# S5 chunks with rows ordered (input, place): inputs by two DMAs, outputs by four writes and four reads

## The chip, the core and the metric

The kernel runs on one core of one Trainium2 chip. The metric is the device time of one execution in microseconds (us). TensorE (PE) multiplies matrices and has its own weight-load track (PEld); VectorE (DVE), ScalarE (ACT) and GpSimd (POOL) do elementwise work. SyncE (SP) issues nearly all DMAs, one after the other: an issue that waits for a semaphore holds up those behind it. Each engine runs its instructions in the order in which they were put down.

## What is computed

One layer of a hybrid decoder for 256 prompt positions and 8 x 8 sample positions, 320 in all. A combined input projection feeds an S5 group and a retention group; both outputs go through one output projection, then a SwiGLU block. All in f32. The S5 part, which the change touches:

```python
    lam_bar = jnp.exp(lam_dt)
    b_bar = ((lam_bar - 1.0) / lam)[..., None] * b
    ug = uf.reshape(n, l, S5_GROUPS, S5_GROUP)
    bu = jnp.einsum('nlgh,gph->lngp', ug.astype(jnp.complex64), b_bar)
    bu = bu.at[0].add(lam_bar[None] * x0)
    _, xs = lax.associative_scan(_lin_combine, (a, bu), axis=0)
    y = jnp.einsum('lngp,ghp->nlgh', xs, c).real.reshape(n, l, S5_WIDTH)
    y = y + d.astype(f32) * uf
    y = jax.nn.gelu(y)
    y = y * jax.nn.sigmoid(y @ w_glu.astype(f32) + b_glu.astype(f32))
```

There are 64 groups of 16 channels; each group drives 64 complex states.

## The kernel before

**Matmuls.** Every large product is made of three f32r passes: weights are split into `hi` (rounded) and `lo` (the rest), activations likewise, and PE adds hi x hi, hi x lo, lo x hi (L143, L144, L145 in `gemm`; L161 to L163 in `gemm_late`). `wload` brings a block of weights, 128 x 1024: a DMA into `raw` on SP (L130), the cast to `hi` on ACT (L131), the subtraction to `lo` on DVE (L133). `raw`, `hi` and `lo` have three buffers each in the first part of the kernel, so a block's load waits until the `lo` three blocks earlier is made.

**Stages.** The input projection (up to about 343 us) has the retention heads and the S5 chunks woven into it. Then come the output projection for retention, the GLU of S5, the output projection for S5, and from about 490 us on the feed-forward block.

**Order.** PE and POOL run in the order of the code (L924): a clock with estimated costs (`clk`, `spawn`, `run_due`) decides there where a chunk's next part is put between matmuls. DVE, ACT and SP are ordered by a scheduler, which uses priorities (weight loads and PSUM evacuations come first) and its own estimates of when things are ready.

**One S5 chunk** (`s5_chunk`, eight of them, each of 128 channels, i.e. eight groups). Positions are taken in blocks of four (CH = 4), so there are 80 blocks (NC). The rows (partitions) of the operands are pairs of an input channel of the group (16, `h`) and a place in the block (4, `e`, `t` or `s`). Before, the order of a row is (place, input): place is the slower index.

- `up_` (ACT, L588) is the chunk's input regrouped; it is written to DRAM (`via`, L591) and read back with eight DMAs (L595) into `kst`, one for each half and place.
- `bl` and `cl` (DVE) are products of the raw B and C matrices (`raw_bc`) with powers of the state's multiplier (`gpc`, `lpc`). `gpc` is made once by ACT (`s5_powers`, L491 and L492).
- PE transposes `bl` into `bst`, multiplies `kst` with it into PSUM `pb`, and `bl` with `cl0` into `pk_`, from which ACT copies one column block of `toe` (L649). Six DMAs inside SBUF (L653) shift it by one, two and three places and complete the matrix `toe` of the block's inner effects.
- `s5_scan` (DVE) runs the recurrence over blocks and leaves `xp`.
- PE multiplies `toe` with `kst` and `cl` with `xp` into `py`; ACT and DVE evacuate it into `ev`. One DMA writes `ev` to DRAM (`back`, L682); eight DMAs read it into `yc` (L687) in the channels' own order.
- `y1` (DVE, L691; the profile shows it at the helper's line L182, `y<-u,vec,yc`) adds the direct term. Then come Square, Identity and Tanh on ACT (L693, L694, L696) with two more DVE operations, and the result goes back to `u32`, where the GLU stage finds it.

ACT is also what normalises the retention heads' outputs (`on`, L804), after DVE's statistics (L787, L788) and a chain of small POOL operations.

Of the kernel before, what the change touches and what calls it, by code (L numbers as in the profile page):

```python
# [12 lines left out]
F32 = mybir.dt.float32  # L13
# [4 lines left out]
ADD, SUB, MUL = ALU.add, ALU.subtract, ALU.mult  # L18
PSUM = bass.MemoryType.PSUM

P = 128
# [11 lines left out]
CH = 4  # L33
NCP = NP // CH
NC = N // CH
# [9 lines left out]
def hybrid_kernel(ctx, tc, xT, w_in, w_in4, w_out, w_glu, w_fi, w_fo, vecs, s5p, bc, x0,  # L45
# [24 lines left out]
    o = 0  # L70
# [34 lines left out]
    def tr(out, in_):  # L105
        m = in_.shape[0]
        pe.transpose(out, in_, ident[:m, :m])
        clk.now += 0.12
# [68 lines left out]
    def tt(out, a, b, op):  # L177
        dve.tensor_tensor(out, a, b, op)  # L178
        return out
# [305 lines left out]
    def s5_powers():  # L485
        for q in range(2):
            for d in range(2):
                o = lpc[:, :, q, 4 * d:4 * d + 4]
                act.mul(o, lp[:, q].rearrange("p e (c j) -> p c j e", j=4), -1.0 if d > q else 1.0)
                o = gpc[:, :, q, 4 * d:4 * d + 4]  # L490
                act.copy(o[:, :, :, 0], ff[:, q].rearrange("p (c j) -> p c j", j=4))  # L491
                act.copy(o[:, :, :, 1:], gp[:, q].rearrange("p e (c j) -> p c j e", j=4))  # L492

    def s5_turns(ec, es):
        pool.memset(e18[:, :, 0, :, 0:1], 1.0)
# [87 lines left out]
    def s5_chunk(c):  # L583
        js = slice(4 * c, 4 * c + 4)
        cl, cl0, xp, d0 = cls_[c % 2], cl0s[c % 2], xps[c % 2], d0s[c % 2]

        up_ = s5.tile([P, CH, NC], F32, name="up_", tag="up_", bufs=2)
        act.copy(up_, u32[:, c].rearrange("p (c s) -> p s c", s=CH))  # L588

        via = drm.tile([4, 2, 16, CH, NC], F32, name="via", tag="via", bufs=2)  # L590
        sp.dma_start(via.rearrange("j g h s c -> (j g h) (s c)"), up_.rearrange("p s c -> p (s c)"))  # L591
        kst = s5.tile([P, 4, NC], F32, name="kst", tag="kst", bufs=2)
        for i in range(2):
            for e in range(CH):
                sp.dma_start(kst[64 * i + 16 * e:64 * i + 16 * e + 16],  # L595
                             via[2 * i:2 * i + 2, :, :, CH - 1 - e].rearrange("q g h c -> h (q g) c"))

        raw = raws[c]
        for q in range(2):
            for g in range(2):  # L600
                act.mul(cl0[64 * g:64 * g + 64, q, :, 16 * g:16 * g + 16],
                        raw[64 * g:64 * g + 64, 1, 4 * q:4 * q + 4], 1.0 - 2.0 * q)
        with tc.issue_after(rot_t["values"].ins):
            act.copy(d0[:, :, :, 1:], r4[:, js].unsqueeze(1).unsqueeze(3).to_broadcast([P, 2, 4, NCP - 1]))
        shm = [P, 8, CH, 16]
        for w_, pc in ((0, gpc), (1, lpc)):
            m1, m2 = (s5.tile(shm, F32, name=f"m{q}", tag=f"m{q}", bufs=1) for q in range(2))
            b_ = raw[:, w_].unsqueeze(2).to_broadcast(shm)
            tt(m1, b_, pc[:, c, 0].unsqueeze(3).to_broadcast(shm), MUL)
            tt(m2, b_, pc[:, c, 1].unsqueeze(3).to_broadcast(shm), MUL)  # L610
            if w_ == 0:

                bl = s5.tile([P, 2, 2, 2, CH, 16], F32, name="bl", tag="bl", bufs=1)
                for r, (a, b, op) in enumerate(((m1[:, 0:4], m2[:, 4:8], SUB), (m1[:, 4:8], m2[:, 0:4], ADD))):
                    a, b = (t_.rearrange("p (u q) e h -> p u q (e h)", q=2) for t_ in (a, b))
                    tt(bl[:, r].rearrange("p q u e h -> p u q (e h)"), a, b, op)
                continue
            tt(cl[:, 0], m1[:, 0:4], m2[:, 4:8], SUB)
            tt(cl[:, 1], m1[:, 4:8], m2[:, 0:4], SUB)
        if c:  # L620
            tbl = s5_table(c)
        yield DL["b1"] + (4.0 if c == 0 else 0.0)
        if not c:
            tbl = s5_table(c)
        bst = s5.tile([P, 4, P], F32, name="bst", tag="bst", bufs=1)
        pt = misc("pt")
        for i in range(4):
            tr(pt[:, P * i:P * i + P], bl[:, i // 2, i % 2].rearrange("p u e h -> p (u e h)"))
        with tc.high_priority(offset=EVAC):
            act.copy(bst, pt.rearrange("p (i s) -> p i s", s=P))  # L630
        load_bc(c + 2)
        yield DL["b2"]
        pb = ps_b.tile([P, 2, 512], F32, name="pb", tag="pb", bufs=1)
        for i in range(4):
            for u in range(2):

                for g in range(2):
                    us, gs = slice(64 * u, 64 * u + 64), slice(64 * g, 64 * g + 64)
                    mm(0.04, pb[gs, u, NC * i:NC * i + NC], bst[us, i, gs], kst[us, 2 * (i % 2) + g],
                       start=True, stop=True, tile_position=(64 * u, 64 * g))  # L640
        pk_ = misc("pk_")
        for i in range(2):
            for q in range(2):
                for u in range(2):
                    mm(0.04, pk_[64 * u:64 * u + 64, 32 * i:32 * i + 32],
                       bl[:, q, i, u].rearrange("p e h -> p (e h)"), cl0[:, q, 2 * u + i],
                       start=q == 0, stop=q == 1, tile_position=(0, 64 * u))
        with tc.high_priority(offset=EVAC):
            act.copy(toe[:, :, CH - 1], pk_[:, 0:64].rearrange("p (q h) -> p q h", h=16))  # L649
        for u in range(2):  # L650
            for t in range(CH - 1):
                d = 16 * (CH - 1 - t)
                sp.dma_start(toe[64 * u + d:64 * u + 64, :, t], toe[64 * u:64 * u + 64 - d, :, CH - 1])  # L653
        with tc.high_priority(offset=2 * EVAC if c == 7 else 0):
            s5_scan(c, pb, xp, d0, tbl)
        yield DL["scan"]


        py = ps_b.tile([P, 2, 512], F32, name="py", tag="pb", bufs=1)
        for g in range(2):  # L660
            for u in range(2):
                for i in range(2):
                    us = slice(64 * u, 64 * u + 64)
                    mm(0.04, py[64 * i:64 * i + 64, u, NC * g:NC * g + NC],
                       toe[us, 2 * i + g].rearrange("p t h -> p (t h)"), kst[us, 2 * i + g], start=g == 0,
                       stop=True, tile_position=(64 * u, 64 * i), skip_group_check=True)
        for u in range(2):
            for q in range(2):
                for g in range(2):
                    for i in range(2):  # L670
                        gs = slice(64 * g, 64 * g + 64)
                        mm(0.04, py[64 * i:64 * i + 64, g, NC * (2 + u):NC * (3 + u)],
                           cl[gs, q, 2 * u + i].rearrange("p t h -> p (t h)"), xp[gs, q, 2 * u + i],
                           start=False, stop=q == 1, tile_position=(64 * g, 64 * i), skip_group_check=True)
        ev = s5.tile([P, 2, 2, NC], F32, name="ev", tag="ev", bufs=1)
        with tc.high_priority(offset=EVAC):
            act.copy(ev.rearrange("p u g c -> p u (g c)"), py[:, :, 0:2 * NC])
            tt(ev, ev,
               py[:, :, 2 * NC:4 * NC].rearrange("p g (u c) -> p u g c", c=NC), ADD)

        back = drm.tile([2, CH, 16, 2, 2, NC], F32, name="back", tag="back", bufs=2)
        sp.dma_start(back.rearrange("i t h u g c -> (i t h) (u g c)"), ev.rearrange("p u g c -> p (u g c)"))  # L682
        yc = s5.tile([P, CH, NC], F32, name="yc", tag="yc", bufs=1)
        for j in range(4):
            for g in range(2):
                r = 32 * j + 16 * g
                sp.dma_start(yc[r:r + 16], back[j % 2, :, :, j // 2, g].rearrange("t h c -> h t c"))  # L687
        yield DL["y"]
        y1 = s5.tile([P, N], F32, name="y1", tag="up_", bufs=2)
        y2 = s5.tile([P, N], F32, name="y2", tag="ev", bufs=1)  # L690
        stt(y1.rearrange("p (c s) -> p c s", s=CH), u32[:, c].rearrange("p (c s) -> p c s", s=CH),  # L691
            v("d", c), yc.rearrange("p s c -> p c s"), MUL, ADD)
        act.activation(y2, y1, AF.Square)  # L693
        act.activation(y2, y2, AF.Identity, scale=0.044715, bias=ones[:, 0:1])  # L694
        tt(y2, y2, y1, MUL)
        act.activation(y2, y2, AF.Tanh, scale=float(np.sqrt(2 / np.pi)))  # L696
        stt(u32[:, c], y2, 1.0, y1, ADD, MUL)
        if c == 7:
            s5_state["done"] = True
# [417 lines left out]
    for n in range(KT):  # L1117
# [8 lines left out]
        else:  # L1126
            s = square(n, hp)
# [216 lines left out]
```

## Time and profile before

| | us |
|---|---|
| median of 3 runs | 1434.91 (1433.25 to 1435.58) |
| the profiled execution | 1433.95 |
| its span, first to last instruction | 1432.1 |

The profile is of one execution, so its times are set against 1433.95 and not against the median. Weights and inputs come at a mean of 186 GB/s. The busy share of PE by slices of a fortieth of the span is 0.9 or more in all but the last:

```profile
PE   9999999999999999999999999999999999999996
...
DVE  7978887777567647776677546777644767644554
ACT  7645555554355433333333333333333333333452
POOL 7530022110000010000001000001000000000001
PEclk9999999999999999999999999999999999999998
DMA  8555555556544466675666446757445765444442
```

Each digit is tenths. The S5 chunks lie in slices 2 to 11. Matmuls are pipelined, so the durations of neighbouring rows overlap: two full matmuls start 0.147 us apart and are shown with 0.31 us each.

### The profile page before, as it was taken

To read this page: it belongs to the slowest core of one execution; us is meant where nothing else is said; L and a number is where in the kernel's file an instruction comes from. 1 tells how busy PE (TensorE), PEld (TensorE's weight loads), DVE (VectorE), ACT (ScalarE), POOL (GpSimd) and SP (SyncE) were. 2 spreads that over 40 slices of the span, in tenths; PEclk is the share of its full clock that TensorE was granted. 3 is DMA by queue.
4 is the path that set the end of the run, shared out by engine and by line. 5 is a ranking of instruction groups with operands and counts; after the bars stand their busy time and mean duration, and the time that the engine had idled before them with its cause. 6 is when DMAs were issued, how large, how long until landed. Compare 5 with 4: busy or idle time off the path is not lost.

```text
span 1432.1 us, 26209 instructions
## 1 busy us (share of the span) xinstructions
PE 1418.1 (99%) x10394; PEld 1407.6 (98%) x10394; DVE 954.6 (67%) x1853; ACT 598.8 (42%) x944; POOL 125.1 (9%) x193
## 2 busy tenths in 40 slices
PE   9999999999999999999999999999999999999996
PEld 9999999999999999999999999999999999999996
DVE  7978887777567647776677546777644767644554
ACT  7645555554355433333333333333333333333452
POOL 7530022110000010000001000001000000000001
PEclk9999999999999999999999999999999999999998
DMA  8555555556544466675666446757445765444442
GB/s 285 175 172 161 165 167 165 169 160 208 162 156 152 152 210 228 221 250 205 239 217 228 128 150 234 247 202 254 151 152 185 256 225 183 153 127 156 148 148 108
DMA packets 101803, 266.87 MB, mean 186 GB/s; under 512 B 27312, under 2 KB 41776, under 8 KB 101680
## 3 DMA queue, kind: packets, MB, share of 16 engines
q1 hardware_dynamic: 101536, 264.94, 55.7%
q8 instruction: 81, 1.33, 0.4%
q14 instruction: 42, 0.34, 0.1%
q10 hardware_dynamic: 144, 0.26, 0.1%
HBM read 254.24 MB, written 10.52 MB: 185 GB/s over the span
## 4 chain that ended last, share of the span: by engine, by line
PE 71%; DVE 1%; issue 0%; ACT 0%; DVEq 0%
PE ps_fu L144 7%; PE ps_fu L143 7%; PE ps_fo L143 7%; PE ps_fo L144 7%; PE ps_fo L145 7%; PE ps_fu L145 7%; PE ps_fg L144 7%; PE ps_fg L143 7%; PE ps_fg L145 7%; PE ps_o L145 1%; PE ps_o L143 1%; PE ps_o L144 1%; PE ps_g L144 1%; PE ps_g L145 1%; PE ps_g L143 1%; DVE x L178 0%
## 5 line engine op out<-in xcount | busy, mean ns | idle before, releaser
L131 ACT CAST hi<-raw 128x1024 fp32r<-128x1024 f32 (+1 forms) x416 | 402.2, 968 | 697.4 <-PE ps_fo L144 189.0
L133 DVE TENSOR_TENSOR lo<-raw,hi 128x1024 fp32r<-128x1024 f32 (+1 forms) x416 | 467.5, 1124 | 314.9 <-ACT hi L131 312.4
L144 PE MATMUL ps_fo<-alo,hi 128*128 128x320 f32 x704 | 217.5, 309 | 0.0
L143 PE MATMUL ps_fg<-hhi,hi 128*128 128x320 f32 x704 | 217.5, 309 | 0.0
L143 PE MATMUL ps_fo<-ahi,hi 128*128 128x320 f32 x704 | 217.5, 309 | 0.0
L145 PE MATMUL ps_fo<-ahi,lo 128*128 128x320 f32 x704 | 217.5, 309 | 0.0
L144 PE MATMUL ps_fu<-hlo,hi 128*128 128x320 f32 x704 | 217.4, 309 | 0.0
L145 PE MATMUL ps_fg<-hhi,lo 128*128 128x320 f32 x704 | 217.4, 309 | 0.0
L143 PE MATMUL ps_fu<-hhi,hi 128*128 128x320 f32 x704 | 217.4, 309 | 0.0
L144 PE MATMUL ps_fg<-hlo,hi 128*128 128x320 f32 x704 | 217.4, 309 | 0.0
L145 PE MATMUL ps_fu<-hhi,lo 128*128 128x320 f32 x704 | 217.4, 309 | 0.0
L143 PE MATMUL ps_p<-xhi,hi 128*128 128x320 f32 x560 | 177.3, 317 | 0.0
L145 PE MATMUL ps_p<-xhi,lo 128*128 128x320 f32 x560 | 173.0, 309 | 0.0
L144 PE MATMUL ps_p<-xlo,hi 128*128 128x320 f32 x560 | 172.8, 309 | 0.0
L144 PEld LDWEIGHTS ps_fg<-hlo,hi 128*128 128x128 f32 x704 | 132.4, 188 | 0.0
L143 PEld LDWEIGHTS ps_fo<-ahi,hi 128*128 128x128 f32 x704 | 132.4, 188 | 0.0
L143 PEld LDWEIGHTS ps_fu<-hhi,hi 128*128 128x128 f32 x704 | 132.4, 188 | 0.0
L144 PEld LDWEIGHTS ps_fu<-hlo,hi 128*128 128x128 f32 x704 | 132.4, 188 | 0.0
L145 PEld LDWEIGHTS ps_fo<-ahi,lo 128*128 128x128 f32 x704 | 132.4, 188 | 0.0
L145 PEld LDWEIGHTS ps_fu<-hhi,lo 128*128 128x128 f32 x704 | 132.4, 188 | 0.0
L143 PEld LDWEIGHTS ps_fg<-hhi,hi 128*128 128x128 f32 x704 | 132.3, 188 | 0.0
L145 PEld LDWEIGHTS ps_fg<-hhi,lo 128*128 128x128 f32 x704 | 132.3, 188 | 0.0
(441 smaller groups left out, 2066.6 us busy)
## 6 DMA issues: line engine op xcount, KB each, us to landing
raw<-w_fi SPq DMA_DIRECT2D x176, 512.0 KB, 4.1
raw<-w_in SPq DMA_DIRECT2D x79, 512.0 KB, 4.1
raw<-w_fo SPq DMA_DIRECT2D x64, 512.0 KB, 3.5
raw<-w_out SPq DMA_DIRECT2D x32, 512.0 KB, 3.7
hi<-vd SPq DMA_DIRECT2D x32, 512.0 KB, 5.5
lo<-vd SPq DMA_DIRECT2D x32, 512.0 KB, 5.2
raw<-w_fo SPq DMA_DIRECT2D x64, 192.0 KB, 2.4
rt<-r SPq DMA_DIRECT2D x8, 512.0 KB, 5.3
```

The source lines that it names most:

```text
L131: cast = act.copy(hi[:, :m], raw[:, :m])
L133: last_lo[0] = dve.tensor_tensor(lo[:, :m], raw[:, :m], f(hi[:, :m]), SUB)
L143: pe.matmul(ps, hi, xhi[:, k], start=k == 0, stop=False)
L144: pe.matmul(ps, hi, xlo[:, k], start=False, stop=False)
L145: pe.matmul(ps, lo, xhi[:, k], start=False, stop=k == nk - 1)
```

## The change

The order of a row becomes (input, place): the place is the faster index. Then a half of `kst` is one DMA, `yc` is read in four DMAs, and for that `back` is laid out by (half, place, upper, group, input) and written by four DMAs. A shift by places is now a step between rows four apart, so the copies inside `toe` go over every fourth row (32 of them), still six a chunk. `gpc` gets the places in reverse order, with both halves (`d`) in one copy. The sizes of all matmuls, transposes and DVE operations stay.

```diff
-                o = gpc[:, :, q, 4 * d:4 * d + 4]
-                act.copy(o[:, :, :, 0], ff[:, q].rearrange("p (c j) -> p c j", j=4))
-                act.copy(o[:, :, :, 1:], gp[:, q].rearrange("p e (c j) -> p c j e", j=4))
+            for e in range(CH):
+                src = gp[:, q, e - 1] if e else ff[:, q]
+                act.copy(gpc[:, :, q, :, CH - 1 - e].rearrange("p c (d j) -> p c d j", j=4),
+                         src.rearrange("p (c j) -> p c j", j=4).unsqueeze(2).to_broadcast([P, 8, 2, 4]))
...
         for i in range(2):
-            for e in range(CH):
-                sp.dma_start(kst[64 * i + 16 * e:64 * i + 16 * e + 16],
-                             via[2 * i:2 * i + 2, :, :, CH - 1 - e].rearrange("q g h c -> h (q g) c"))
+            sp.dma_start(kst[64 * i:64 * i + 64], via[2 * i:2 * i + 2].rearrange("q g h s c -> (h s) (q g) c"))
...
-        shm = [P, 8, CH, 16]
         for w_, pc in ((0, gpc), (1, lpc)):
+            dm = 3 - w_
+            shm = [P, 8, CH, 16] if w_ else [P, 8, 16, CH]
...
-            b_ = raw[:, w_].unsqueeze(2).to_broadcast(shm)
-            tt(m1, b_, pc[:, c, 0].unsqueeze(3).to_broadcast(shm), MUL)
+            b_ = raw[:, w_].unsqueeze(dm).to_broadcast(shm)
+            tt(m1, b_, pc[:, c, 0].unsqueeze(5 - dm).to_broadcast(shm), MUL)
...
-                bl = s5.tile([P, 2, 2, 2, CH, 16], F32, name="bl", tag="bl", bufs=1)
+                bl = s5.tile([P, 2, 2, 2, 16, CH], F32, name="bl", tag="bl", bufs=1)
...
-        for u in range(2):
-            for t in range(CH - 1):
-                d = 16 * (CH - 1 - t)
-                sp.dma_start(toe[64 * u + d:64 * u + 64, :, t], toe[64 * u:64 * u + 64 - d, :, CH - 1])
+        for t in range(CH - 1):
+            for i in range(t + 1):
+                sp.dma_start(toe[i::CH, :, t], toe[i + CH - 1 - t::CH, :, CH - 1])
...
-        back = drm.tile([2, CH, 16, 2, 2, NC], F32, name="back", tag="back", bufs=2)
-        sp.dma_start(back.rearrange("i t h u g c -> (i t h) (u g c)"), ev.rearrange("p u g c -> p (u g c)"))
+        back = drm.tile([2, CH, 2, 2, 16, NC], F32, name="back", tag="back", bufs=2)
+        for u in range(2):
+            for g in range(2):
+                sp.dma_start(back[:, :, u, g].rearrange("i t h c -> (i t) h c"), ev[:, u, g])
         yc = s5.tile([P, CH, NC], F32, name="yc", tag="yc", bufs=1)
         for j in range(4):
-            for g in range(2):
-                r = 32 * j + 16 * g
-                sp.dma_start(yc[r:r + 16], back[j % 2, :, :, j // 2, g].rearrange("t h c -> h t c"))
+            sp.dma_start(yc[32 * j:32 * j + 32], back[j % 2, :, j // 2].rearrange("t g h c -> (g h) t c"))
```

PE's and POOL's instructions stand in the same order as before. On SP, DVE and ACT the scheduler puts some elsewhere.

DVE around chunk 4's output, before (`t`, `ends`, `w`, `v` are chunk 5's recurrence, `mv` the statistics of a retention head, `lo` a weight block):

```order
L788 BN_AGGR mv<-st 128x2 x2
L178 TENSOR_TENSOR t_3735<-pb,tb 128x2x128 x2
L178 TENSOR_TENSOR t_3736<-pb,tb 128x2x128 x2
L178 TENSOR_TENSOR ends<-pb,lx_133 128x2x16
L178 TENSOR_TENSOR w<-t_3735,t_3736 128x256 x2
L133 TENSOR_TENSOR lo<-raw,hi 128x1024
L178 TENSOR_TENSOR ends<-pb,lx_133 128x2x16
L571 SCALAR_TENSOR_TENSOR w<-d_137,w 128x512
L178 TENSOR_TENSOR v_3750<-w,tb 128x512
L182 SCALAR_TENSOR_TENSOR y_3663<-u_119,vec,yc 128x320
L178 TENSOR_TENSOR v_3751<-w,tb 128x512
L133 TENSOR_TENSOR lo<-raw,hi 128x1024
```

The same place now (lines behind the edit are one lower or higher than before):

```order
L182 SCALAR_TENSOR_TENSOR y_3622<-u_119,vec,yc 128x320
L787 BN_AGGR mv<-st 128x2
L178 TENSOR_TENSOR y_3623<-y_3623,y_3622 128x320
L182 SCALAR_TENSOR_TENSOR u_119<-y_3623,y_3622 128x320
L178 TENSOR_TENSOR t_3694<-pb,tb 128x2x128 x2
L178 TENSOR_TENSOR t_3695<-pb,tb 128x2x128 x2
L178 TENSOR_TENSOR ends<-pb,lx_133 128x2x16
L178 TENSOR_TENSOR w<-t_3694,t_3695 128x256 x2
L133 TENSOR_TENSOR lo<-raw,hi 128x1024
L178 TENSOR_TENSOR ends<-pb,lx_133 128x2x16
L572 SCALAR_TENSOR_TENSOR w<-d_137,w 128x512
L178 TENSOR_TENSOR v_3709<-w,tb 128x512
```

Chunk 4's output operations `y` and `u` stand ahead of chunk 5's recurrence and one `lo` earlier, with the last aggregate of the statistics behind the first of them; after the last row follow the other `v`, both `xp` and then the next `lo`. On ACT the Square, Identity and Tanh move likewise: the three `on` stand between Identity and Tanh.

SP at chunk 4's output, before (a `raw` row is a weight load):

```order
L682 DMA back<-ev 128x320
L130 DMA raw<-w_in 128x1024
L550 DMA raw_bc<-bc 128x256
L687 DMA yc<-back 16x4x80 x3
L130 DMA raw<-w_in 128x1024
L687 DMA yc<-back 16x4x80 x5
```

Now:

```order
L683 DMA back<-ev 8x16x80 x4
L867 DMA mk<-masks 128x384
L686 DMA yc<-back 32x4x80 x3
L130 DMA raw<-w_in 128x1024
L686 DMA yc<-back 32x4x80
```

The reads and the writes they wait for stand closer together: one weight load lies between the reads, and none between the writes and the first read.

SP at chunk 7's shifts of `toe`, before:

```order
L130 DMA raw<-w_out 128x1024
L687 DMA yc<-back 16x4x80 x3
L653 DMA toe<-toe 16x4x16
L653 DMA toe<-toe 32x4x16
L653 DMA toe<-toe 48x4x16
L130 DMA raw<-w_out 128x1024
L653 DMA toe<-toe 16x4x16
L653 DMA toe<-toe 32x4x16
L653 DMA toe<-toe 48x4x16
```

Now:

```order
L683 DMA back<-ev 8x16x80 x4
L814 DMA rp_o<-rp 128x128
L686 DMA yc<-back 32x4x80 x4
L130 DMA raw<-w_out 128x1024 x3
L652 DMA toe<-toe 32x4x16 x6
L130 DMA raw<-w_out 128x1024 x2
```

All six shifts stand together, and chunk 6's reads (`yc`) stand three weight loads ahead of them.

More of the change, by code (lines that the diff above doesn't have):

```diff
@@ L604, in s5_chunk @@
             act.copy(d0[:, :, :, 1:], r4[:, js].unsqueeze(1).unsqueeze(3).to_broadcast([P, 2, 4, NCP - 1]))
-        shm = [P, 8, CH, 16]
         for w_, pc in ((0, gpc), (1, lpc)):
+            dm = 3 - w_
+            shm = [P, 8, CH, 16] if w_ else [P, 8, 16, CH]
             m1, m2 = (s5.tile(shm, F32, name=f"m{q}", tag=f"m{q}", bufs=1) for q in range(2))
-            b_ = raw[:, w_].unsqueeze(2).to_broadcast(shm)
-            tt(m1, b_, pc[:, c, 0].unsqueeze(3).to_broadcast(shm), MUL)
-            tt(m2, b_, pc[:, c, 1].unsqueeze(3).to_broadcast(shm), MUL)
+            b_ = raw[:, w_].unsqueeze(dm).to_broadcast(shm)
+            tt(m1, b_, pc[:, c, 0].unsqueeze(5 - dm).to_broadcast(shm), MUL)
+            tt(m2, b_, pc[:, c, 1].unsqueeze(5 - dm).to_broadcast(shm), MUL)
             if w_ == 0:
-                bl = s5.tile([P, 2, 2, 2, CH, 16], F32, name="bl", tag="bl", bufs=1)
+                bl = s5.tile([P, 2, 2, 2, 16, CH], F32, name="bl", tag="bl", bufs=1)
                 for r, (a, b, op) in enumerate(((m1[:, 0:4], m2[:, 4:8], SUB), (m1[:, 4:8], m2[:, 0:4], ADD))):
-                    a, b = (t_.rearrange("p (u q) e h -> p u q (e h)", q=2) for t_ in (a, b))
-                    tt(bl[:, r].rearrange("p q u e h -> p u q (e h)"), a, b, op)
+                    a, b = (t_.rearrange("p (u q) h s -> p u q (h s)", q=2) for t_ in (a, b))
+                    tt(bl[:, r].rearrange("p q u h s -> p u q (h s)"), a, b, op)
                 continue
@@ L627, in s5_chunk @@
         for i in range(4):
-            tr(pt[:, P * i:P * i + P], bl[:, i // 2, i % 2].rearrange("p u e h -> p (u e h)"))
+            tr(pt[:, P * i:P * i + P], bl[:, i // 2, i % 2].rearrange("p u h s -> p (u h s)"))
         with tc.high_priority(offset=EVAC):
@@ L645, in s5_chunk @@
                     mm(0.04, pk_[64 * u:64 * u + 64, 32 * i:32 * i + 32],
-                       bl[:, q, i, u].rearrange("p e h -> p (e h)"), cl0[:, q, 2 * u + i],
+                       bl[:, q, i, u].rearrange("p h s -> p (h s)"), cl0[:, q, 2 * u + i],
                        start=q == 0, stop=q == 1, tile_position=(0, 64 * u))
```

## The prediction

> **What bounds the kernel now.** I read the head of the page first, then TensorE (PE) by stage, then what PE waited for.
>
> ```profile
> span 1432.1 us, 26209 instructions
> ## 1 busy us (share of the span) xinstructions
> PE 1418.1 (99%) x10394; PEld 1407.6 (98%) x10394; DVE 954.6 (67%) x1853; ACT 598.8 (42%) x944; POOL 125.1 (9%) x193
> ```
> ```profile
> 45.00:376.00 331.00, 329.97 (x3006) 322.71 (x3006) 263.82 (x549) 175.02 (x378) 63.23 (x114) 1.00 0.54 168
> ```
>
> PE is idle for 14.0 us in all (1432.1 - 1418.1). The second row is the window from 45 to 376 us, in which all eight S5 chunks run (columns: length, then busy time of PE, PEld, DVE, ACT, POOL, then granted clock, DMA share, GB/s). PE is idle there for 331.00 - 329.97 = 1.03 us, at the full clock. The edit changes neither the number nor the shape nor the order of PE's instructions. So what it can give is at most these 1.03 us, 0.07% of the time. What it can take has no such bound: it depends on whether something that PE needs comes late.
>
> What PE waits for, by engine and line (total, times, longest; the three of interest):
>
> ```profile
> PE py L102 <- DMA toe<-toe: 0.5, 1, 0.5
> PE py L957 <- ACT hi L947: 0.5, 1, 0.5
> PE pss L102 <- POOL ksp L886: 0.5, 1, 0.5
> ```
> ```profile
> 342.80 0.43 PE L102 MATMUL py<-kst,toe 64*64 64x80 f32 x10 [0.50 <-DMA toe<-toe]
> ```
>
> Of the waits only the first belongs to a DMA that the edit touches: chunk 7's output matmuls stood 0.50 us until the small shift copies inside `toe` had landed. The others are the start-up and a POOL copy before the first chunk has outputs.
>
> **The DMAs, seven fewer a chunk.** The DMA list of before (KB each, median us from issue to landing):
>
> ```profile
> kst<-via SPq DMA_DIRECT2D x64, 20.0 KB, 3.4
> back<-ev SPq DMA_DIRECT2D x8, 160.0 KB, 3.6
> yc<-back SPq DMA_DIRECT2D x64, 20.0 KB, 3.5
> ...
> toe<-toe SPq DMA_DIRECT2D x16, 12.0 KB, 2.8
> ```
>
> Per chunk `kst` goes from 8 to 2, `yc` from 8 to 4, `back` from 1 to 4, `toe` stays at 6: 24 DMAs with `via` become 17, and 56 issues go in all. At 0.44 us (1.32 for three, row below) that is 24.6 us of SP time. SP is not the bound: the weight loads that share its queue wait for their buffers anyway, and PE waits for none of them. I cost this at nothing. A `kst` DMA of 64 partitions does not occur before; it moves 80 KB, between the 20 KB in 3.4 us and the 160 KB in 3.6 us, so 3.4 to 3.6. No `kst` is issued later than before. Nothing.
>
> **ACT's coefficient copies.** Eight copies stay eight and move the same 512 elements a partition, now 64 each.
>
> ```profile
> 58.52 0.61 ACT L491 COPY gpc<-ff 128x32 f32<-128x32 f32 x4 [1.30 <-DVE ff L178]
> ```
> ```profile
> 64.75 0.91 ACT L492 COPY gpc<-gp 128x96 f32<-128x96 f32 x4
> ```
>
> A copy of 64 lies between 0.15 (0.61/4) and 0.23 (0.91/4) us. Six stand now where four stood at 64.75: 0.9 to 1.4 us against 0.91, so 0 to +0.5 on ACT, once. PE had no wait in that place, and later casts catch up. I take 0. The DVE products and the transposes keep their sizes; only the order of their elements changes. Nothing, with no row to the contrary.
>
> **Chunk 7's shifts.** SP before:
>
> ```profile
> 333.80 1.88 SPq L653 DMA_DIRECT2D toe<-toe  x3
> 338.29 0.36 SPq L130 DMA_DIRECT2D raw<-w_out  x1
> 338.75 2.54 SPq L653 DMA_DIRECT2D toe<-toe  x3
> ```
>
> Three of the six copies stood behind a weight load that waited for its buffer, so the last was issued 341.29 - 0.85 = 340.4. Now all six stand together ahead of it, and chunk 6's `yc` reads no longer stand right before them. At 1.88/3 = 0.63 us the six take 3.8 us; begun at 333.8 the last starts at 336.9 and lands by 339.7 (2.8 later). PE comes there at 341.95 or later (342.80 less the 0.50 and the matmuls before it), so 2 us are to spare. The wait of 0.50 goes. Ends: 0 and -0.5; I take -0.5.
>
> **The outputs, where the risk is.** The scheduler believes that `yc` comes sooner. So it puts the first step of the output, `y1` on DVE (L182, it reads `yc`), one to three weight blocks earlier, and its Square and Tanh on ACT with it. If `yc` has not landed, DVE and ACT stand, and behind them stand the weight casts (`hi` on ACT, `lo` on DVE) that PE needs. Before, `y1` never waited. The tightest place that I find is chunk 4; SP, DVE and ACT there:
>
> ```profile
> 252.17 0.35 SPq L130 DMA_DIRECT2D raw<-w_in  x1
> 252.58 0.42 SPq L550 DMA_DIRECT2D raw_bc<-bc  x1
> 253.09 1.32 SPq L687 DMA_DIRECT2D yc<-back  x3
> ```
> ```profile
> 248.02 0.48 DVE L178 TENSOR_TENSOR ev<-ev,py 128x320 f32<-128x320 f32 x1
> ...
> 257.37 0.30 DVE L788 BATCH_NORM_AGGREGATE mv<-st 128x2 f32<-128x6 f32 x2
> 260.19 1.42 DVE L178 TENSOR_TENSOR t<-pb,tb 128x256 f32<-128x256 f32 x4 [2.52 <-PE pb L102]
> 261.52 0.18 DVE L178 TENSOR_TENSOR ends<-pb,lx 128x32 f32<-128x32 f32 x1
> 261.65 0.76 DVE L178 TENSOR_TENSOR w<-t,t 128x256 f32<-128x256 f32 x2
> 264.05 1.23 DVE L133 TENSOR_TENSOR lo<-raw,hi 128x1024 fp32r<-128x1024 f32 x1 [1.64 <-ACT hi L131]
> 265.19 0.19 DVE L178 TENSOR_TENSOR ends<-pb,lx 128x32 f32<-128x32 f32 x1
> 265.29 1.22 DVE L571 TENSOR_TENSOR_SCAN w<-d,w 128x512 f32<-128x512 f32 x1
> 266.54 0.69 DVE L178 TENSOR_TENSOR v<-w,tb 128x512 f32<-128x512 f32 x1
> 267.15 0.79 DVE L182 SCALAR_TENSOR_TENSOR y<-u,vec,yc 128x320 f32<-128x320 f32 x1
> 267.86 0.68 DVE L178 TENSOR_TENSOR v<-w,tb 128x512 f32<-128x512 f32 x1
> 268.46 1.21 DVE L133 TENSOR_TENSOR lo<-raw,hi 128x1024 fp32r<-128x1024 f32 x1
> ...
> 271.55 0.78 DVE L178 TENSOR_TENSOR xp<-v,v 128x252 f32<-128x252 f32 x2
> ```
> ```profile
> 260.74 1.16 ACT L804 ACTIVATE on<-po,gy 128x128 f32<-128x128 f32 x3 [3.67 <-POOL gy L798]
> ```
> ```profile
> 272.32 0.47 ACT L696 ACTIVATE y<-y 128x320 f32<-128x320 f32 x1
> ```
> ```profile
> 269.28 0.31 PE L145 MATMUL ps_p<-xhi,lo 128*128 128x320 f32 x1
> ```
> ```profile
> 272.80 0.31 PE L145 MATMUL ps_p<-xhi,lo 128*128 128x320 f32 x1
> ```
>
> The two PE rows are the first uses of the two `lo` blocks in the DVE rows (the 56th and 57th loaded through L130, counted along both engines): they are ready at 265.28 and 269.67, 4.0 and 3.1 us early. Now step by step. `ev` ends at 248.50. Four `back` writes at 0.44: the last is issued at 249.8 and lands 3.6 later, 253.4. Three `yc` reads wait for it on SP, with the weight load of 252.17 behind them: 254.7; that load, 255.1; the fourth read, issued then, lands 3.5 later at 258.6. So the load goes 2.9 us later; its cast came only on the block of 268.46, so it has room. DVE reaches `y1` at about 257.5 and waits 1.1 us; `y1` ends at 259.4. Behind it now stands the last aggregate of the group norm: 259.6 instead of 257.67. POOL needs 260.74 - 257.67 = 3.1 us from there to `on` on ACT: 262.7; three `on` 263.8; Tanh behind them 264.3; DVE's `u` (0.49) 264.8; `t`, `ends`, `w` (2.36) 267.1; `lo` (1.23) 268.4, against 269.28. Then `ends`, scan, both `v`, `xp` (3.56) 271.9, and the next `lo` (1.21) 273.1, against 272.80. Rows on DVE overlap a little: the six from 264.05 to 268.46 sum to 4.80 in 4.41 us, 0.065 each. For the thirteen from `u` on I take 0.8 off: 272.3, in time by 0.5.
>
> So the margin here falls from 3.1 to about half a microsecond; PE loses nothing if `yc` lands as it did, and up to 0.7 us if one takes 4.7 (1.2 more), the longest below:
>
> ```profile
> DMA to landing us min/median/max: 1.6/3.5/4.7
> ```
>
> I take +0.2 for this chunk and 0 for the others, where the same order has blocks ready longer before their use or fewer steps between `y1` and the cast.
>
> A rule of the Trainium skill speaks against the four writes. "DMA: Bandwidth & Descriptors", Rules for kernel authors, says that a DMA's outermost dimension limits the engines it is spread over; a `back` write has 8 there instead of 128. Its Specifications ask for 512 B a row for full rate; a row falls from 1280 to 320 B. No transfer of before has this form, so no run here shows it; by these the landing would come later than 3.6 us, which is the rival of the late landing below.
>
> **Sum.** -0.5 (chunk 7's shifts) + 0.2 (chunk 4) + 0 = -0.3 us. The profiled execution took 1433.95 us, the median shown is 1434.91 (1433.25 to 1435.58), 0.96 more. 1433.95 - 0.3 = 1433.65, as a median 1434.6.
>
> **Rivals.** *Late landing, slower.* `back` or `yc` lands a few us later than its neighbours did, because of the new form or the traffic (DMA share 0.54 in this stretch). It costs PE from 0.5 us on at chunk 4. If `back` takes twice its 3.6 us, chunk 4 loses 3.6 - 0.5 = 3.1. Other chunks had some 3 to 4 us more of ready work than they use, by the two margins above; if two of them lose half as much, the sum is 6.2 and the time 1434.4 + 6.2 = 1440.6. For: the margin above is small, DVE is busy for 264 of 331 us there. Against: every DMA of these sizes took 2.8 to 3.6 us. Chance 0.12.
>
> *All small waits go, faster.* With fewer issues SP loads weights sooner, and the 1.03 us of idle time vanishes: 1434.91 - 1.03 = 1433.9. That is still within 0.2%. To be faster than that, 2.9 us, PE would need to run its matmuls closer together, of which no row speaks. Chance of that 0.03; of 1433.9 itself, 0.15.
>
> *A moved wait, small.* The wait at chunk 7 stays or chunk 4 loses about a microsecond: 1435.5 to 1436. Chance 0.2. The forecast near 1434.6 has the remaining 0.5.
>
> 0.2% (2.9 us) is about what a measurement of this kernel can tell from no change. Faster 0.03; same 0.15 + 0.2 + 0.5 = 0.85; slower 0.12. The range goes from 1432.8 (0.45 under the lowest run shown, for the idle time that may go) to 1438.0 (3.4 over the forecast, chunk 4 with a doubled landing).
>
> **What would show it.** Right: PE's wait for `toe` is gone from its list; PE's idle time from 45 to 376 us is between 0.5 and 1.5 us; DVE has waits for `yc` at L182 of 0 to 3 us, which it had none of; the last `yc` read of chunk 4 is issued near 255. Wrong: PE waits on `lo` or `hi` between 120 and 340 us, or on `vT` or `on`, which share ACT with the Square; `back` taking over 6 us to land; SP standing on `back` for more than 3 us a chunk with a weight load behind it that PE then waits for.

## The result, and the profile after

| | median (range) of the runs, us | before beside it, us | ratio, 95% interval |
|---|---|---|---|
| the change | 1436.84 (1435.69 to 1439.15) | 1434.42 (1433.25 to 1435.58) | 1.0019 [1.0011, 1.0028] |
| the change, second time | 1436.84 (1435.7 to 1441.62) | 1434.36 (1433.33 to 1436.1) | 1.0023 [1.0014, 1.0033] |

The change makes the kernel about 2.4 us slower: less than 0.2%, but both intervals lie above 1. The profiled execution of the changed kernel took 1435.69 us, with a span of 1433.9. The head of its page and the window from 45 to 376 us, in the columns shown for before:

```profile
PE 1418.7 (99%) x10394; PEld 1407.2 (98%) x10394; DVE 955.6 (67%) x1853; ACT 598.1 (42%) x944; POOL 123.0 (9%) x193
```
```profile
45.00:376.00 331.00, 328.52 (x2991) 320.24 (x2990) 263.92 (x548) 173.80 (x377) 62.37 (x114) 1.00 0.55 168
```

TensorE is busy for the same time in all (1418.7 against 1418.1). In the window it is idle for 331.00 - 328.52 = 2.48 us, before 1.03. (Both traces have 10394 matmul records. The 15 fewer in the window run after its end: by the comparison below the changed kernel is 0.6 us ahead at its start and 1.8 us behind at its end.) What TensorE waits for now:

```profile
PE pss L102 <- POOL ksp L885: 1.6, 2, 1.1
...
PE ps_o L162 <- DVE r4b L178: 0.4, 1, 0.4
...
PE ps_p L145 <- DVE lo L133: 0.3, 1, 0.3
```

The wait for `toe` is gone. Two new ones are there, for a `lo` block and for `r4b` (the split gated output of a retention head, input of the output projection), and the one for `ksp` comes twice. VectorE's list has what was not there before:

```profile
DVE y L182 <- DMA yc<-back: 9.5, 4, 4.5
```

`y1`, the first step of a chunk's output, stands and waits for the rows `yc`. Its wait of 2.0 us in chunk 0 is put down to `toe`, which it does not read; with that it is 11.5 us in five chunks. The same in place, chunk 1 on VectorE (a bracket is the idle time before a row, and what ended it):

```profile
150.75 0.48 DVE L182 SCALAR_TENSOR_TENSOR retp<-pn,vec,sg 128x256 f32<-128x256 f32 x1
155.75 0.78 DVE L182 SCALAR_TENSOR_TENSOR y<-u,vec,yc 128x320 f32<-128x320 f32 x1 [4.53 <-DMA yc<-back]
156.46 1.21 DVE L133 TENSOR_TENSOR lo<-raw,hi 128x1024 fp32r<-128x1024 f32 x1
```

Before, that `y1` ran at 161.54, behind two more casts.

**Where TensorE lost the time.** Matmuls stand in the same order in both kernels, so the same matmul can be looked up in both traces and its starts compared. The first large one behind the second `ksp` product, of before and after:

```profile
171.29 0.39 PE L143 MATMUL ps_p<-xhi,hi 128*128 128x320 f32 x1
```
```profile
171.82 0.49 PE L102 MATMUL pss<-qsp,ksp 128*128 128x128 f32 x2 [0.41 <-POOL ksp L885]
172.07 0.39 PE L143 MATMUL ps_p<-xhi,hi 128*128 128x320 f32 x1
```

It is 0.78 us later; the large matmul behind the `ksp` product near 86 us was 0.11 later (85.90 and 86.01). So 0.67 us were lost between. Done for all 3,008 first-pass matmuls (hi x hi) of L143 and L161, the difference stays level for long stretches and jumps at few places; jumps under 0.12 us are left out. From 360 us to the end it stays level within 0.02 us. What lies ahead of this matmul at 86 us is left out too. Start-up differed by up to 1.6 us between executions (34.47 to 36.05 for the first such matmul). The first wait for `ksp`, 1.1 of the 1.6 us in the list above, goes with the execution and not with the change: its step is +0.67 and +0.08 in two executions of the change, and +0.80 and -0.03 in two of one other kernel (e3 and e9 below).

Positive is later than before:

| kernel | 171 (`ksp`) | 247 (`ksp`) | 269 to 290 (`lo`) | 343 (`toe`) | 348 (`r4b`) | sum | median less that of before |
|---|---|---|---|---|---|---|---|
| the change | +0.67 | | +0.75 | -0.84 | +1.05 | +1.63 | +2.42 |
| the change, second time | +1.14 | | +1.23 | -0.84 | +1.48 | +3.01 | +2.48 |

So the losses are at three places, and one gain at the shifts of `toe`. A step is larger than the idle time that the profile lists with it (0.67 against 0.41 at 171, 1.05 against 0.44 at 348). The rows of the other two losses:

```profile
274.07 0.42 PE L145 MATMUL ps_p<-xhi,lo 128*128 128x320 f32 x1 [0.32 <-DVE lo L133]
...
348.87 0.41 PE L162 MATMUL ps_o<-r4b,hi 128*128 128x320 f32 x1 [0.44 <-DVE r4b L178]
```

**At 171**, `ksp` is POOL's copy of a retention head's sample keys; it stands on POOL behind the product `kvf` of the same keys. POOL before, then after:

```profile
165.47 0.43 POOL L884 TENSOR_TENSOR kvf<-k__2327,kdt 128x64 f32<-128x64 f32 x1 [9.22 <-DVE k__2327 L178]
165.84 0.70 POOL L886 COPY ksp<-k__2327 128x64 f32<-128x64 f32 x1
```
```profile
168.62 2.77 POOL L883 TENSOR_TENSOR kvf<-k__2307,kdt 128x64 f32<-128x64 f32 x1 [9.05 <-DVE k__2307 L178]
171.34 0.43 POOL L885 COPY ksp<-k__2307 128x64 f32<-128x64 f32 x1
```

The keys leave VectorE 3.15 us later, behind chunk 1's wait, and the product takes 2.77 us, not 0.43. Both were needed. With 0.43 us the copy would have ended near 169.5, and TensorE asked for it at 171.41 (171.82 less its wait); this is worked out only. That a slow product at the old place costs nothing is shown by e3 below, which has no loss here:

```profile
166.11 3.17 POOL L883 TENSOR_TENSOR kvf<-k__2309,kdt 128x64 f32<-128x64 f32 x1 [9.35 <-DVE k__2309 L178]
```

**At 348**, VectorE's rows before, then after (`finp` and `fins` are the final states of S5, outputs that no later matmul reads):

```profile
344.19 1.23 DVE L133 TENSOR_TENSOR lo<-raw,hi 128x1024 fp32r<-128x1024 f32 x1
345.33 0.49 DVE L178 TENSOR_TENSOR r4b<-retp,r4b 128x320 fp32r<-128x320 f32 x1
...
346.53 1.30 DVE L178 TENSOR_TENSOR r4b<-retp,r4b 128x320 fp32r<-128x320 f32 x3
...
348.30 0.69 DVE L178 TENSOR_TENSOR fins<-fins,ends 128x512 f32<-128x512 f32 x1
```
```profile
344.94 0.18 DVE L178 TENSOR_TENSOR finp<-xp 128x32 f32<-128x32 f32 x1
345.06 0.42 DVE L178 TENSOR_TENSOR fins<-xp 128x256 f32<-128x256 f32 x1
345.40 0.48 DVE L178 TENSOR_TENSOR sg<-ps_p,rbc 128x320 f32<-128x320 f32 x1
345.80 0.68 DVE L178 TENSOR_TENSOR fins<-fins,ends 128x512 f32<-128x512 f32 x1
346.40 1.22 DVE L133 TENSOR_TENSOR lo<-raw,hi 128x1024 fp32r<-128x1024 f32 x1
347.54 0.48 DVE L178 TENSOR_TENSOR retp<-retp,sg 128x320 f32<-128x320 f32 x1
347.94 0.48 DVE L178 TENSOR_TENSOR ev<-ev,py 128x320 f32<-128x320 f32 x1
348.33 1.69 DVE L178 TENSOR_TENSOR r4b<-retp,r4b 128x320 fp32r<-128x320 f32 x4
```

The last part of the final states stood behind `r4b`; now it stands ahead of it, 1.28 us in these rows.

### The profile page after: what moved, and what is told of

It reads as the page before. It is cut to its first block, busy times and chain, and to the rows that moved or that the text cites. A ratio compares the mean times of both kernels' runs of the same rounds, so it can differ in the third digit from the quotient of the medians.

```text
span 1433.9 us, 26118 instructions
## 1 busy us (share of the span) xinstructions
PE 1418.7 (99%) x10394; PEld 1407.2 (98%) x10394; DVE 955.6 (67%) x1853; ACT 598.1 (42%) x944; POOL 123.0 (9%) x193
## 4 chain that ended last, share of the span: by engine, by line
PE 71%; DVE 0%; issue 0%; ACT 0%; DVEq 0%
PE ps_fo L143 7%; PE ps_fu L143 7%; PE ps_fu L144 7%; PE ps_fo L144 7%; PE ps_fo L145 7%; PE ps_fu L145 7%; PE ps_fg L143 7%; PE ps_fg L144 7%; PE ps_fg L145 7%; PE ps_o L145 1%; PE ps_o L144 1%; PE ps_o L143 1%; PE ps_g L144 1%; PE ps_g L145 1%; PE ps_g L143 1%; DVE x L178 0%
## 5 line engine op out<-in xcount | busy, mean ns | idle before, releaser
L143 PE MATMUL ps_fg<-hhi,hi 128*128 128x320 f32 x704 | 217.5, 309 | 0.0
L143 PE MATMUL ps_fo<-ahi,hi 128*128 128x320 f32 x704 | 217.5, 309 | 0.0
L143 PE MATMUL ps_fu<-hhi,hi 128*128 128x320 f32 x704 | 217.4, 309 | 0.0
L143 PE MATMUL ps_p<-xhi,hi 128*128 128x320 f32 x560 | 177.3, 317 | 0.0
L143 PEld LDWEIGHTS ps_fo<-ahi,hi 128*128 128x128 f32 x704 | 132.4, 188 | 0.0
L143 PEld LDWEIGHTS ps_fu<-hhi,hi 128*128 128x128 f32 x704 | 132.4, 188 | 0.0
L143 PEld LDWEIGHTS ps_fg<-hhi,hi 128*128 128x128 f32 x704 | 132.3, 188 | 0.0
```

The source lines that it names most:

```text
L143: pe.matmul(ps, hi, xhi[:, k], start=k == 0, stop=False)
```

## The experiments

Theory A: the new DMAs cost nothing by themselves. The scheduler, which believes in an earlier `yc`, moves `y1` ahead on VectorE; there it waits, and what queues behind it (casts, keys, `r4b`) comes late. Rival B: the new writes and reads are the cost. Rival C: the inputs' part of the change is. Each kernel had five rounds of timing; each is compared with the kernel before that ran beside it.

**e1, `y1` held back.** The changed kernel, with `y1` of chunks 0 to 6 held behind the weight cast that it followed before. `HOLD` numbers the casts; the new wait stands on VectorE itself. In the trace `y1` has its old place among the casts in chunks 0, 1, 4 and 5; it comes one cast later in chunks 2 and 3, and one earlier in 6.

```diff
+                los_.append(last_lo[0])
...
+        while c < 7 and len(los_) <= HOLD[c]:
+            yield 0.4
-        stt(y1.rearrange("p (c s) -> p c s", s=CH), u32[:, c].rearrange("p (c s) -> p c s", s=CH),
+        with tc.issue_after(los_[HOLD[c] if c < 7 else -1].ins):
+            stt(y1.rearrange("p (c s) -> p c s", s=CH), u32[:, c].rearrange("p (c s) -> p c s", s=CH),
```

> The changed kernel, with y1 on VectorE (for chunks 0 to 6) held behind the weight block behind which it stood before the change; all DMAs as changed. Theory A (the outputs' first step was moved ahead and stands there waiting for yc, and casts and the k of a retention head queue behind it): VectorE's waits for yc fall from 9.5 us to under 1.5 us, TensorE's waits on ksp near 171 us, on lo near 273 us and on r4b near 348 us go, time 1433.7 to 1434.6, about that of before or 0.5 under. Rival B (the new DMAs themselves cost, by late landing or by traffic that slows the weight loads): nothing of that, time stays at 1436.8.

Measured: 1434.93 (1433.67 to 1436.08), ratio 0.9998 [0.999, 1.0007]. VectorE has no wait for `yc` in its list, TensorE none for `lo` or `r4b`. All DMAs of the change are in, and of 2.42 us above the kernel before 0.17 are left, so rival B falls as the cause of the measured loss. The median is 0.3 us above the range that was expected. One loss is new, at 247 us; it is taken up behind e8.

**e2, the outputs alone, and e3, the inputs alone.** e2 is the kernel before with only the last hunk of the diff (`back`, `yc`); e3 is the change without that hunk:

```diff
-        back = drm.tile([2, CH, 2, 2, 16, NC], F32, name="back", tag="back", bufs=2)
-        for u in range(2):
-            for g in range(2):
-                sp.dma_start(back[:, :, u, g].rearrange("i t h c -> (i t) h c"), ev[:, u, g])
+        back = drm.tile([2, CH, 16, 2, 2, NC], F32, name="back", tag="back", bufs=2)
+        sp.dma_start(back.rearrange("i t h u g c -> (i t h) (u g c)"), ev.rearrange("p u g c -> p (u g c)"))
```

> The kernel of before with the outputs' edit alone (four writes, four reads); VectorE's order is then exactly that of the changed kernel. Theory A: the whole loss, 1436.8 to 1437.5 (the wait for toe at chunk 7 may remain, +0.5), with waits of VectorE for yc of 6 to 11 us. Rival B: the same. Rival C (the inputs' edit costs, through fewer and larger kst reads, gpc or toe): the time of before, 1434.4.

> The changed kernel with the outputs' DMAs of before (one write, eight reads). Theory A and rival B: 1433.9 to 1434.6, no wait of VectorE for yc, the wait for toe near 342 us gone. Rival C: 1436 to 1437.

Measured: e2 1437.96 (1436.71 to 1444.13), ratio 1.0029 [1.0019, 1.0038]; e3 1433.5 (1432.82 to 1433.73), ratio 0.9991 [0.9982, 0.9999]. The outputs' part carries the whole loss, the inputs' part none: rival C falls. VectorE's 1853 rows stand in e2 in the same order as in the change. e2 came out 0.5 us above its range, with waits for `yc` of 12.0 us instead of 6 to 11.

e3 came out 0.4 us below its range, and not free of waits: `y1` stands one or two casts earlier than before in chunks 2 to 6, and in chunk 2 it waits 1.1 us for `yc`. TensorE loses nothing by that, so a wait of VectorE costs only where something stands behind it that TensorE is short of. (VectorE's list has 5.2 us more for `yc`, ahead of a `lo` at 325.70; the kernel before has the same gap there, 5.24 us, put down to ACT.)

TensorE's waits in e2:

```profile
PE ps_o L162 <- DVE r4b L178: 2.3, 1, 2.3
...
PE ps_p L145 <- DVE lo L133: 0.6, 1, 0.6
```

The wait for `toe` is gone in both, so either part alone takes it away: in e3 the six shifts stand together at 332.91, in e2 at 336.59, and only before were they parted by a weight load.

**e4, `ksp` first.** The changed kernel with POOL's copy of the keys ahead of the product.

```diff
+        pool.tensor_copy(ksp[:, 64 * (h % 2):64 * (h % 2) + 64], k_[:, NP:N])
...
-        pool.tensor_copy(ksp[:, 64 * (h % 2):64 * (h % 2) + 64], k_[:, NP:N])
```

> The changed kernel with GpSimd's copy into ksp ahead of its product into kvf. If the wait near 171 us is the late k passed on by a slow GpSimd operation (2.8 us), ksp is ready 2.5 us earlier, TensorE's wait on ksp falls from 1.6 us to under 0.6 us and the time by 0.5 to 1 us, to about 1436. If a later wait takes its place (the lo block behind it), the time stays at 1436.8.

Measured: 1436.53 (1435.17 to 1440.72), ratio 1.0014 [1.0005, 1.0023], which does not part it from the change. The jump at 171 is gone, but the losses at `lo` and `r4b` were larger in its profile (1.54 and 2.12), with 0.87 more near 310, at another wait for `ksp` (0.60). So TensorE's list still has 1.7 us for `ksp`, where under 0.6 was expected. POOL's rows say something else: the operation that comes first is the slow one, whichever it is.

```profile
168.68 2.71 POOL L883 COPY ksp<-k__2307 128x64 f32<-128x64 f32 x1 [9.04 <-DVE k__2307 L178]
171.35 0.58 POOL L884 TENSOR_TENSOR kvf<-k__2307,kdt 128x64 f32<-128x64 f32 x1
```

**e5, early `y1` without its wait.** `y1` keeps the place on VectorE that the change gave it, but in chunks 0 to 6 it reads the tile `kst`, long loaded, in place of `yc`. The returned rows of these chunks are left out of the output. `traced()` gives the cast that is to precede `y1`. In the trace `y1` has the place of the change in all chunks but 2, where it runs six casts earlier (at 160.93 us), not one; it waited for nothing there in the change either. The two VectorE operations that follow `y1` come earlier as well, and a few rows around them change places.

```diff
+        with tc.issue_after(traced()[0]):
...
-            v("d", c), yc.rearrange("p s c -> p c s"), MUL, ADD)
+                v("d", c), (kst if c < 7 else yc).rearrange("p s c -> p c s"), MUL, ADD)
```

> The changed kernel with the first step of S5's output, y1, at the place on VectorE that the change gave it (chunk 2's one cast earlier), but in chunks 0 to 6 it reads the earlier tile kst in place of the returned rows yc. So it has nothing to wait for: the output leaves out the returned rows of seven of the eight chunks. Theory A1 (it is the waiting of y1 for yc, and what queues behind it on VectorE): the 9.5 us of VectorE waits for yc go, and with them TensorE's wait for ksp at 171 us and the one for lo at 273 us; TensorE's idle time between 45 and 376 us falls from 2.48 to 1.2 to 1.7, and the time to 1434.7 to 1435.9. The wait for r4b near 348 us stays if it comes from the order alone, and goes if it comes from the backlog. Rival A2 (the work moved ahead, y1 and what follows it, delays the casts by itself, with no wait in it): idle time stays at 2.2 to 2.7 and the time at 1436.3 to 1437.2.

Measured: 1435.16 (1433.95 to 1439.99), ratio 1.0008 [1.0, 1.0017]. The jumps at 171 and at 273 are gone, the one at 348 is there (1.22). So the wait makes the first two losses (A1), and the order makes the third; A2 holds for 348 alone. TensorE's idle time in the window, 331.00 - 329.28 = 1.72 us, is just above what A1 gave. The size of the loss at 348 does not go by the order alone: with the same order and 12.0 us of waits, e2 lost 2.89 there.

**e6, final states behind `r4b`.** The changed kernel, its early `y1` and the waits included, with the block of `finp` and `fins` after the last `r4b`:

```diff
-    newscr(2)
-    finp = s5.tile([P, 2, NPAIR], F32, name="finp", tag="m0", bufs=1)
...
-    sp.dma_start(s5s_o, fins)
...
+    with tc.issue_after(last_r.ins):
+        newscr(2)
+        finp = s5.tile([P, 2, NPAIR], F32, name="finp", tag="m0", bufs=1)
...
+        sp.dma_start(s5s_o, fins)
```

> The changed kernel with the final states' VectorE work (finp, fins) placed behind the last cast of r4b; nothing else differs, the early y1 and its waits stay. Theory A': the loss near 348 us comes from these 1.3 us of work ahead of r4b: TensorE's wait for r4b (1.0 in the changed kernel's profile) goes, its idle time falls to 1.3 to 1.8, and the time to 1435.2 to 1436.0. Rival: r4b is late because all of VectorE's work is late by then: the wait stays at 0.7 or more and the time within 0.5 us of 1436.8.

Measured: 1436.23 (1434.49 to 1437.04), ratio 1.0009 [1.0, 1.0017]. Theory A' holds: TensorE's wait for `r4b` is gone (0.4 us in the list of the change, with a step of 1.05), those for `ksp` and `lo` are still there, with 0.7 us each.

The median is 0.2 us above what was expected; the sum of the steps went from between 1.63 and 3.01 to 0.92.

**e7, inputs alone with the final states late, and e8, all repairs.** e7 is e3 with the edit of e6. e8 is the whole change with the edits of e1, e6 and e4.

> The changed inputs with the outputs' DMAs as before, and the final states' VectorE work behind the last cast of r4b. If that work still costs something where the outputs are the old ones, 1432.8 to 1433.3; if not, as the changed inputs alone: 1433.2 to 1433.8.

> The whole change, with y1 held behind the casts of lo that it stood behind before in chunks 0 to 6, the final states' work behind the last cast of r4b, and POOL's copy ksp ahead of its product kvf. If the change's DMAs cost nothing and only the order does, this is as good as the changed inputs alone: 1433.0 to 1434.3. If the fewer and other writes and reads of the outputs cost something by themselves, it stays at 1434.7 or above.

Measured: e7 1433.48 (1432.59 to 1434.28), ratio 0.9993 [0.9984, 1.0001], so late final states add nothing where the outputs are the old ones. e8 1434.17 (1433.08 to 1435.15), ratio 0.9996 [0.9987, 1.0004]. The whole change with these three places mended is no slower than before, but it stays 0.7 us above e7, and e1 1.4 above e3. Their profiles have one loss that e3 and e7 have not, at 247. POOL and TensorE in e1:

```profile
242.72 5.52 POOL L889 TENSOR_TENSOR kvf<-k__3364,kdt 128x64 f32<-128x64 f32 x1 [4.57 <-DVE k__3364 L181]
248.19 0.23 POOL L891 COPY ksp<-k__3364 128x64 f32<-128x64 f32 x1
```
```profile
248.47 0.49 PE L102 MATMUL pss<-qsp,ksp 128*128 128x128 f32 x2 [0.66 <-POOL ksp L891]
```

In e8 the copy, there in front, took 5.46 us at the same place, so putting it first gains 0.2 us at most (steps of 0.93 and 0.74). Here the slow operation on POOL alone makes the wait: the keys came no later than in e3 (242.72 against 243.02 for the start of `kvf`), where it took 2.50 us and `ksp` was ready at 245.9. In e1 and e8 `y1` of chunk 3 runs one cast later than before, and its last two VectorE operations (`y<-y,y` and `u<-y,y`) fall among the rows beside this product, where the kernel before and e3 do not have them. That this is what made the product longer fits the rows in the last section; no run shows it.

**e9 and e10, the inputs alone and the change once more.**

> The changed inputs with the outputs' DMAs as before, once more beside the changed kernel. If it beats the kernel before by the removed wait for toe and nothing else, 0.4 to 1.2 us under the kernel before and 2.5 to 3.8 under the changed kernel. If its earlier gain was chance, level with the kernel before.

> The changed kernel once more. Theory A (waits at three places, which the order on VectorE sets): the losses near 171, 273 and 348 us are there again, in sum 1.5 to 3.0 us of TensorE's time, less 0.84 at the shifts; time 1436.0 to 1437.2. If the losses of its first profile were of that execution alone, their places or sizes differ by more than 1 us each.

Measured: e9 1433.27 (1432.32 to 1434.44), ratio 0.9993 [0.9984, 1.0002]; e10 is the second row of the first table. The three places and the gain came again, so they are not of one execution; the losses sum to 3.85 us, more than the 3.0 expected. e9 is 1.09 us under before and 3.57 under the change. Together with e3 and e7, three timings of the inputs alone (e7 with its late final states) are 1.1 to 1.3 us under before; the interval of one of them leaves 1 out, barely.

The steps of all, as in the first such table:

| kernel | 171 | 247 | 269 to 290 | 343 | 348 | sum | median less that of before |
|---|---|---|---|---|---|---|---|
| e1 `y1` held | | +0.93 | | -0.84 | | +0.09 | +0.17 |
| e2 outputs alone | | | +1.05 | -0.84 | +2.89 | +3.10 | +3.20 |
| e3, e7, e9 inputs alone | | | | -0.84 | | -0.84 | -1.26, -1.12, -1.09 |
| e4 `ksp` first (+0.87 at 310) | | | +1.54 | -0.84 | +2.12 | +3.69 | +1.77 |
| e5 no wait (+0.14 at 310) | | | | -0.84 | +1.22 | +0.52 | +0.56 |
| e6 final states late | +0.52 | | +1.24 | -0.84 | | +0.92 | +1.63 |
| e8 all repairs | | +0.74 | | -0.84 | | -0.10 | -0.43 |

A sum is of one profiled execution, a median of 11 or more; but for e4 they agree within 0.8 us.

## Why the prediction was wrong

The place of the risk was right; its size was not, and with it the sign. The sum was -0.5 + 0.2 + 0; in its place stand -0.84 and losses of 2.5 to 3.9 us. That 1436.84 lies in the stated range of 1432.8 to 1438.0 all the same is luck: the upper end was worked out from a `back` that takes twice its time, and that did not come. Nor was 2.9 us the least that can be told from no change: the intervals reach 1.2 to 1.4 us to either side.

- **What bounds the kernel: right.** TensorE, with little to win and no bound on what can be lost.
- **DMA issues, ACT's copies, DVE products: right,** 0. e3 has all but the outputs' issues and loses nothing; these are in e8, whose one loss against e7 is the step at 247.
- **Chunk 7's shifts: right,** as far as the wait went (0.50 in the list). The step measured 0.84: from the first of these matmuls to the next stage TensorE took 1.83 us before (341.95 to 343.78) and 0.99 in e3 (342.46 to 343.45), and the list shows only 0.50 of that as idle. So the 1.03 us of idle time were no upper bound of what the waits cost. The gain does not need the inputs' edit: e2 has it with the old shifts, which stand together there too.
- **`back` and `yc`: no late landing.** What SP stood for `back` in all (total, times, longest), and chunk 4's rows on SP and VectorE:

```profile
SPq L686 <- DMA back<-ev: 5.0, 8, 1.6
```
```profile
250.88 2.56 SPq L683 DMA_DIRECT2D back<-ev  x4
...
254.69 1.28 SPq L686 DMA_DIRECT2D yc<-back  x3
...
256.49 0.42 SPq L686 DMA_DIRECT2D yc<-back  x1
```
```profile
260.29 0.77 DVE L182 SCALAR_TENSOR_TENSOR y<-u,vec,yc 128x320 f32<-128x320 f32 x1 [1.97 <-DMA yc<-back]
```

The first read went out 3.8 us after the first write's issue, where I had 4.9 (253.4 less 248.5), though the four issues took 0.64 us each, not 0.44. SP never stood over 1.6 us for `back`, where 3 us a chunk was to be the sign. The rival of the late landing falls. The Trainium skill's "DMA: Bandwidth & Descriptors", Rules for kernel authors, limits such a write to 8 engines by its outermost dimension; no run here shows on how many it ran, and whatever that costs is within these 3.8 us.

- **The term of chunk 4: right place, wrong size.** Taken +0.2, measured +0.75 and +1.23. `ev` ended at 250.85, not 248.50, since VectorE, which had run from 231 us up to it without a wait, was already late; `y1` started 3.8 us after the last read's issue, not 3.5; it waited 1.97 us, not 1.1. The chain behind it took what was worked out, and a margin of 0.5 us did not survive a `y1` that ended 1.7 us later (261.06, not 259.4). Small slips of the working changed nothing: the rows from `u` on are eleven and not thirteen, so 0.7 us had to go off and not 0.8; the weight load goes 2.5 us later, not 2.9; the landing times of 2.8 to 3.6 us were medians; a doubled landing gives 1434.4 + 3.1 = 1437.5, not 1438.0.
- **The step that failed: "0 for the others, where the same order has blocks ready longer before their use or fewer steps between `y1` and the cast".** It looked at casts alone, and at how long a cast has room, not at whether the rows have come when VectorE reaches `y1`. In chunk 1 VectorE came to `y1` 4.53 us too soon, and behind it stood the keys, which reach TensorE by POOL (0.67 and 1.14 us lost at 171). And the prediction took the order for changed only around `y1`: near 348 the final states had come ahead of `r4b`, at 1.05 and 1.48 us (e6: with these moved back the wait is gone). For neither had I read the order.
- **The list of what would show it** told right from wrong: idle time of 2.48 us where 0.5 to 1.5 was right (0.67 of it at 86 us, which goes with the execution), a wait of TensorE for `lo` at 274, and 9.5 us of waits for `yc` where 0 to 3 was right.

What stays open: why the scheduler put the final states ahead; its changed estimates of `yc` are the likely reason, which no run tests. And how much of the remaining 0.7 to 1.4 us between e8 or e1 and the inputs alone belongs to anything but the step at 247 (0.74 and 0.93).

## What to carry to other kernels

A shorter DMA list can cost time by what a scheduler does with it: compare the whole order of each in-order engine, not only around the edited lines, and for each operation moved ahead ask when its data lands and what queues behind it, through every engine that feeds the bottleneck. Where two halves of a change can be separated, time them apart: here the half that saves the most DMAs (the inputs) is by itself the best of the versions timed. A wait of an engine that is not the bottleneck is no loss in itself: ask what stands behind it. A margin of half a microsecond at the end of a long chain did not hold here.

## What the runs showed of the hardware

One POOL product of 128x64 elements took from 0.3 to 5.5 us. `kvf` in the eight heads of the kernel before: 0.39, 0.32, 0.32, 0.43, 2.44, 1.90, 2.51, 0.43; of e1 at 242.72: 5.52. VectorE in e1 meanwhile:

```profile
242.56 0.42 DVE L181 TENSOR_TENSOR cl<-m,m 128x256 f32<-128x256 f32 x1
242.89 0.48 DVE L181 TENSOR_TENSOR y<-y,y 128x320 f32<-128x320 f32 x1
243.29 1.22 DVE L135 TENSOR_TENSOR lo<-raw,hi 128x1024 fp32r<-128x1024 f32 x1
244.43 1.42 DVE L181 TENSOR_TENSOR e<-e 128x256 f32<-128x256 f32 x4
245.77 0.75 DVE L181 TENSOR_TENSOR tb<-e,e 128x256 f32<-128x256 f32 x2
246.44 0.48 DVE L185 SCALAR_TENSOR_TENSOR u<-y,y 128x320 f32<-128x320 f32 x1
246.84 1.22 DVE L135 TENSOR_TENSOR lo<-raw,hi 128x1024 fp32r<-128x1024 f32 x1
247.98 0.48 DVE L181 TENSOR_TENSOR ev<-ev,py 128x320 f32<-128x320 f32 x1
```

Each row starts before the one ahead has ended, and all up to `ev` read both their operands from SBUF; POOL's product ends at 248.24, 0.26 us after `ev`, whose second operand `py` is in PSUM, has begun. The same product in e3 starts at 243.02 and ends at 245.52, 0.14 us after the start of a VectorE row that stands behind a gap of 0.03 us (244.59 + 0.76 = 245.35, the next at 245.38):

```profile
244.59 0.76 DVE L178 TENSOR_TENSOR cl<-m,m 128x256 f32<-128x256 f32 x2
245.38 1.47 DVE L178 TENSOR_TENSOR e<-e 128x256 f32<-128x256 f32 x4
```

This is so for all: of the 13 such products that took 1.9 us or more in the kernel before, the change, e1 and e3, 12 end 0.14 to 0.15 us after the start of the first VectorE row behind a gap (0.03 us), and the 13th, that of e1 above, met no gap. That VectorE's rows without a gap hold POOL up is what the two engines' times suggest; no run here took them apart.

The Trainium skill's "SBUF — State Buffer", Who interferes with whom, has a rule of this kind: a VectorE instruction with two SBUF inputs contends with a GpSimd instruction that reads SBUF, for a lock that one of them holds alone, and the order of issue decides which of the two is blocked. The trace agrees in kind, but by its rows the hold lasts over a whole run of such instructions, up to 5.5 us, and not over one (1.2 us for the longest, `lo`). So the time of a small POOL product seems to go by where it falls among VectorE's rows. It does not simply grow as VectorE loses its waits: the eight products took 8.7 us in the kernel before, 13.4 in e1, and 5.8 in e5, where `y1` has no wait either.
